# Conditioning sums with two buffers, then in pieces of 512 columns, and a mixing matrix turned in place: a two-layer hybrid encoder step on one core

## The chip, the core and the metric

The kernel runs on one core of a Trainium2 chip. The metric is the device time of one launch in microseconds (us); lower is better. TensorE (PE) does matmuls and transposes, VectorE (DVE) and ScalarE (ACT) do elementwise work, and SyncE (SP) and ScalarE each issue transfers on a queue of their own. PE accumulates in PSUM; everything else lives in on-chip buffers ("tiles") that are taken in turn from pools with a fixed number of buffers.

## What is computed

One step of a two-layer encoder for 1024 prompt rows and 32 sample rows with shared weights. All of it is float32.

```python
for i in range(2):
    mod = silu(c) @ w_ada[i] + b_ada[i]              # (1, 6*1024), one for prompt, one for sample
    sh1, sc1, gt1, sh2, sc2, gt2 = split(mod, 6)
    h = rmsnorm(x, g_norm[i, 0]) * (1 + sc1) + sh1
    if i == 0:                                       # spatial gating, chunks of T = 128 (sample: 32) rows
        u, v = split(gelu(h @ w_in), 2)              # 2048 columns each, 8 groups of 256
        v = rmsnorm(v, g_v)
        s = einsum('gij,bnjgd->bnigd', w_s * mask, v by chunk and group) + b_s
        mix = (u * s) @ w_out
    else:                                            # windowed means of 2, 4, 8, 16 rows, minus the row,
        mix = pool_mixer(h)                          # then a 256 x 256 map per group
    x = x + gt1 * rmsnorm(mix, g_norm[i, 1])
    h = rmsnorm(x, g_norm[i, 2]) * (1 + sc2) + sh2
    x = x + gt2 * rmsnorm(square(relu(h @ w_up[i])) @ w_down[i], g_norm[i, 3])
```

Each layer's `w_ada` is 1024 x 6144, 24 MB, and is read once for two conditioning vectors.

## The kernel before

**Tiles.** The 1056 rows lie transposed (features on partitions) in three tiles of 384, 384 and 288 columns. Large products are made from a high and a low part of each operand: `products` issues three matmuls per term, high x high, high x low and low x high. A weight piece of 128 x 1024 arrives in a `raw` buffer (3 of them), ACT copies its high part `wh` and VectorE subtracts to get `wl` (`do_w`); both take slots of `W` (16 slots, 8 pieces).

**Stages.** First the norms and the first products (`early`). Then the v stage: `v_order` lists 31 products of a 128-row block by a piece of 512 columns of v, 13 of the first two pieces, then 9 each of the third and the fourth. Then the gating stage: `mixes` lists six pairs of groups with the tiles that each runs over; one `sgu_item` per pair and tile (12 in all) makes u for two groups (`up`), gates it (`gate`) and multiplies by the output weights (`down`, held back until the next item's first product). Then both layers' FFN, with the pool mixer's work between.

**The stream.** All weights come in one list, `stream`, in the order in which `add_w`, `add_ada` and `add_x` append them; `some_ada(n)` puts n conditioning items between the weights. `issue` keeps three raw buffers loading, on SP's queue. `weave` runs after each product or so: it takes at most one item off the stream, unless `stream_waits` says that a planner's clock for VectorE (`time["dve"]`) is ahead of that for PE (`time["pe"]`). `need_w` forces everything ahead of a weight that a product needs.

**Conditioning.** The first 16 items go over PE (`do_ada_pe`). The other 80 go over VectorE (`do_ada`): an item is 512 rows by 256 columns of `w_ada`, two items make a slice. For both vectors, VectorE multiplies the rows by `csil` (silu of c) and adds into `aa`, a buffer of 2 x 256 columns of which there is one. The sum over the 128 partitions is PE's: `fold` multiplies by `pick` (a column of ones at a moving place) in four 32-row strips, collects four slices in a PSUM tile, and `fold2` transposes the lot and adds the bias (`ada_finish`). Folds are put off by `defer` and run in `run_deferred`; the first item of a slice forces the fold before it.

**Mixing matrix.** `sgu_group` loads a group's 128 x 128 matrix into `ws` (one buffer), transposes it on PE, copies it to `wt` (three buffers), clears a quarter (the mask), and loads the bias rows into `bs`, all loads on SP. `inputs`, ahead of a group's first products, loads v and scales the matrix by v's norm factors into `wr`.

The instructions of one engine stand in the order that the framework gives them, which isn't always that of the program. Elementwise helpers on VectorE have the line L79.

Of the kernel before, what the change touches and what calls it, by code (L numbers as in the profile page):

```python
# [9 lines left out]
F32 = mybir.dt.float32  # L10
# [24 lines left out]
def tile_stream_encoder_step(  # L35
# [78 lines left out]
    nc.vector.tensor_copy(onesr, one[:, :P])  # L114
    ones = onesr.bitcast(F32)

    pick = const.tile([P, 64], F32, name="pick")
    nc.vector.memset(pick, 0.0)
    nc.vector.memset(pick[:, 31:32], 1.0)
# [94 lines left out]
    def add_ada(l, j):  # L214

        sl, q = j // 2, j % 2
        stream.append(
            (
                "ada",
                (l, sl, q),  # L220
                w_ada[l][q * 512 : (q + 1) * 512, sl * 256 : (sl + 1) * 256].rearrange(
                    "(k p) f -> p k f", p=P
                ),
                (4, 256),
            )
        )

# [71 lines left out]

    def some_ada(n):  # L300
        for _ in range(min(n, len(rest))):
            add_ada(*rest.pop(0))

    for b in range(3):
        add_x(b)
# [34 lines left out]
    wdone = set()  # L340
    raws = {}
    loads = {}
    state = {"issued": 0, "next": 0, "raw": 0, "used": 0}
    deferred = []

    def in_raw(k):
# [84 lines left out]
        defer(fold)  # L431


    def do_ada(l, sl, q, r):
        if q == 0:
            ada_acc[0] = work.tile([P, NV, 256], F32, tag="aa", bufs=1, name=f"aa{l}_{sl}")
        aa = ada_acc[0]
        for c in range(4):
            for v in range(NV):
                w = r[:, c * 256 : (c + 1) * 256]  # L440
                k = csil[:, 4 * q + c, v : v + 1]
                if q == 0 and c == 0:
                    ts(aa[:, v, :], w, k, None, op0=ALU.mult)
                else:
                    stt(out=aa[:, v, :], in0=w, scalar=k, in1=aa[:, v, :], op0=ALU.mult, op1=ALU.add)
        if q == 0:
            return

        i = sl % 4

        def fold():

            if i == 0:
                ada_acc["ps"] = ps_ms(f"ada{l}_{sl}")
            pa = ada_acc["ps"]
            for c in range(4):
                v, h = c // 2, c % 2
                mm(
                    pa[32 * c : 32 * c + 32, :P],
                    pick[:, 31 - i : 63 - i],  # L460
                    aa[:, v, h * P : (h + 1) * P],
                    start=i == 0,
                    stop=i == 3,
                    tile_position=(0, 32 * c),
                    skip_group_check=True,
                )
            if i < 3:
                return
            s = t_m(f"adas{l}_{sl}")
            act(out=s[:, :P], in_=pa[:, :P], func=AF.Copy)  # L470

            def fold2():
                pb = ps_ms(f"adat{l}_{sl}")
                nc.tensor.transpose(pb[:, :P], s[:, :P], ident)
                ada_finish(
                    l,
                    sl - 3,
                    pb[:, :P].rearrange("p (v h m) -> p m h v", v=NV, h=2)[:, 0:4],
                )

            defer(fold2, 0.8)

        defer(fold, 0.3)

    def defer(step, us=None):

# [42 lines left out]
    def stream_step():  # L529

        k = state["next"]
        kind, key, ap, shape = stream[k]
        issue()
        run_deferred(force=kind == "ada" and key[2] == 0)
        r = raws.pop(k)
        if kind == "w":
            do_w(key, r)
        elif kind == "ada":
            (do_ada_pe if k < first_ada else do_ada)(*key, r)
        else:  # L540
            do_x(key, r)
        state["next"] += 1
        if in_raw(k):
            state["raw"] -= 1
        issue()

    def stream_waits():

        kind, key = stream[state["next"]][:2]
        if kind == "w":  # L550
            return bool(fillers) and wpos[key] > state["used"] + 5 and time["dve"] > time["pe"] + 1.0
        if kind == "ada" and deferred and key[2] == 0:
            return True
        return kind == "ada" and time["dve"] > time["pe"] + 0.5

    def need_w(key):
        state["used"] = max(state["used"], wpos[key])
# [3 lines left out]
        return witem[key]  # L561

    def need_ada(l, which):
        k = max(i for i, s in enumerate(stream) if s[0] == "ada" and s[1] == (l, which * 4 + 3, 1))
# [346 lines left out]
    v_order = [(1, 2)]  # L911
    v_order += [(p, b) for p in range(2) for b in range(3, 9)]
    v_order += [(p, b) for p in range(2, 4) for b in range(9)]
    for p, b in v_order:
        ps = ps_dn(f"pv{p}_{b}")
        v_mm(ps, p, b, range(KB))
        v_end(ps, p, b)
        if p == 2 and b < NT:
            with tc.issue_after(loads[("v", 2, 3)]):
                nc.sync.dma_start(xd[b], acc[b][:, :, HALO:])  # L920
        if p == 3 and b % 3 == 2:
            v_rms(b // 3)
        weave()
# [18 lines left out]
            yield False  # L942

    fillers.append(("state", sgu_state()))


    pending = []
# [28 lines left out]


    def sgu_group(g):
        raw = sgu.tile([P, P], F32, tag="ws", bufs=1, name=f"ws{g}")
        nc.sync.dma_start(raw, sgu_w_s[0, g])  # L980
        bb = sgu.tile([P, P], F32, tag="bs", bufs=3, name=f"bs{g}")
        nc.sync.dma_start(bb, sgu_b_s[0, g].partition_broadcast(P))
        pt = ps_ms(f"wsT{g}")
        nc.tensor.transpose(pt[:, :P], raw, ident)
        wt = sgu.tile([P, P], F32, tag="wt", bufs=3, name=f"wt{g}")
        nc.vector.tensor_copy(wt, pt[:, :P])
        nc.vector.memset(wt[64:P, 0:64], 0.0)
        return wt, bb

    def sgu_item(p, t, mix, after):  # L990
        gs, tiles = mixes[p]
# [5 lines left out]
        vls, wrs = {}, {}  # L997

        def inputs(g):
            wt, _ = mix[g]  # L1000
# [221 lines left out]
    def to_pool(st):  # L1222
# [4 lines left out]
        def run():  # L1227
# [269 lines left out]
```

## Time and profile before

| | |
|---|---|
| median of 3 runs | 2222.41 us (2219.92 to 2223.79) |
| the profiled execution's own time | 2220.61 us |
| its span, first to last instruction | 2218.8 us |
| PE busy | 2187.9 us (99%), 13488 matmuls |
| VectorE busy | 1404.1 us (63%) |
| ScalarE busy | 986.4 us (44%) |
| moved by transfers | 312.99 MB, mean 141 GB/s |

Rows of the profile give a start or a window in us from the span's start, a length, the engine, the line of the kernel, the operation, `out<-in` by the program's names, and in brackets the engine's idle time before it with what ended it. PEld is the load of a matmul's stationary side. A float32 matmul appears as two instructions.

### The profile page before, as it was taken

How to read it: one execution, taken by the hardware profiler on the slowest of the kernel's cores; microseconds unless marked ns; L12 is line 12 of the kernel's file. 1: busy time of each engine (PE TensorE's matmuls, PEld its weight loads, DVE VectorE, ACT ScalarE, POOL GpSimd, SP SyncE). 2: the span in 40 equal slices, each digit the busy share in tenths (PEclk: the TensorE clock that was granted, in tenths of full speed). 3: DMA queues.
4: the chain of work that ended last, by engine and by line, in shares of the span. 5: the costliest groups of instructions: out<-in, count | busy, mean ns of one | idle time of the engine just before them, and what ended most of it. 6: DMA issues, size and time to landing. Idle time of an engine off the chain costs nothing.

```text
span 2218.8 us, 33828 instructions
## 1 busy us (share of the span) xinstructions
PE 2187.9 (99%) x13488; PEld 2096.6 (94%) x13488; DVE 1404.1 (63%) x2646; ACT 986.4 (44%) x1675; POOL 0.7 (0%) x6
## 2 busy tenths in 40 slices
PE   7999999999999999999999999999999999999998
PEld 5777899999999999999999999999999999999998
DVE  4755656665869646676757869878765454433375
ACT  4633423133447553223445556666564542313354
POOL 0000000000000000000000000000000000000000
PEclk9999999999999999999999999999999999999999
DMA  8365533244436543334554556665454552312243
GB/s 299 123 199 196 176 112 126 78 148 126 135 98 194 162 143 124 114 109 125 154 170 140 165 162 187 184 190 155 147 162 140 153 154 64 96 29 77 92 124 110
DMA packets 369090, 312.99 MB, mean 141 GB/s; under 512 B 10818, under 2 KB 345098, under 8 KB 368932
## 3 DMA queue, kind: packets, MB, share of 16 engines
q1 hardware_dynamic: 368660, 310.74, 45.1%
q8 instruction: 105, 1.72, 0.3%
q14 instruction: 53, 0.43, 0.1%
q10 hardware_dynamic: 272, 0.10, 0.0%
HBM read 278.95 MB, written 31.84 MB: 140 GB/s over the span
## 4 chain that ended last, share of the span: by engine, by line
PE 92%; DVE 3%; DMA 3%; ACT 1%; issue 0%; SPq 0%; DVEq 0%; ACTq 0%
PE pf L803 11%; PE pf L804 11%; PE pf L805 11%; PE pg L803 11%; PE pg L804 11%; PE pg L805 11%; PE po L803 3%; PE po L804 3%; PE po L805 3%; PE pu L803 3%; PE pu L805 3%; PE pu L804 3%; PE pv L830 2%; PE pv L831 2%; PE pv L832 2%; DVE aa L79 2%
## 5 line engine op out<-in xcount | busy, mean ns | idle before, releaser
L803 PE MATMUL pg<-fh,wh_dn 128*128 128x384 f32 (+1 forms) x1536 | 499.2, 325 | 0.0
L803 PE MATMUL pf<-hh,wh_up 128*128 128x384 f32 (+1 forms) x1536 | 497.6, 324 | 0.6 <-ACT wh_up L372 0.6
L805 PE MATMUL pf<-hh,wl_up 128*128 128x384 f32 (+1 forms) x1536 | 495.8, 323 | 0.6 <-DVE wl_up L79 0.6
L804 PE MATMUL pf<-hl,wh_up 128*128 128x384 f32 (+1 forms) x1536 | 496.3, 323 | 0.0
L804 PE MATMUL pg<-fl,wh_dn 128*128 128x384 f32 (+1 forms) x1536 | 494.4, 322 | 0.0
L805 PE MATMUL pg<-fh,wl_dn 128*128 128x384 f32 (+1 forms) x1536 | 494.1, 322 | 0.0
L79 DVE TENSOR_TENSOR wl_up<-raw,wh_up 128x1024 fp32r<-128x1024 f32 x152 | 185.8, 1223 | 169.8 <-ACT wh_up L372 169.8
L803 PEld LDWEIGHTS pg<-fh,wh_dn 128*128 128x128 f32 x1536 | 288.5, 188 | 4.0 <-issue 2.4
L803 PEld LDWEIGHTS pf<-hh,wh_up 128*128 128x128 f32 x1536 | 288.2, 188 | 2.8 <-issue 1.4
L804 PEld LDWEIGHTS pg<-fl,wh_dn 128*128 128x128 f32 x1536 | 288.6, 188 | 0.7
L805 PEld LDWEIGHTS pf<-hh,wl_up 128*128 128x128 f32 x1536 | 288.2, 188 | 1.0 <-DVE wl_up L79 1.0
L805 PEld LDWEIGHTS pg<-fh,wl_dn 128*128 128x128 f32 x1536 | 288.6, 188 | 0.0
L804 PEld LDWEIGHTS pf<-hl,wh_up 128*128 128x128 f32 x1536 | 288.2, 188 | 0.4
L372 ACT ACTIVATE wh_up<-raw 128x1024 fp32r<-128x1024 f32 x152 | 161.0, 1059 | 281.5 <-PE pf L804 208.1
L79 DVE TENSOR_TENSOR acc<-acc,pg 128x384 f32<-128x384 f32 (+1 forms) x336 | 173.4, 518 | 141.1 <-PE pg L805 140.5
L372 ACT ACTIVATE wh_dn<-raw 128x1024 fp32r<-128x1024 f32 x152 | 161.0, 1060 | 210.6 <-PE pg L804 164.3
L79 DVE TENSOR_TENSOR wl_dn<-raw,wh_dn 128x1024 fp32r<-128x1024 f32 x152 | 185.9, 1223 | 89.3 <-ACT wh_dn L372 89.0
L79 DVE SCALAR_TENSOR_TENSOR aa<-raw,csil,aa 128x256 f32<-128x256 f32 x560 | 231.2, 478 | 1.8 <-DMA raw<-in_w_ada_dram 1.8
L1121 ACT ACTIVATE r<-pf 128x384 f32<-128x384 f32 (+1 forms) x192 | 86.6, 451 | 202.7 <-PE pf L805 199.3
L79 DVE TENSOR_TENSOR fl<-r,fh 128x384 fp32r<-128x384 f32 (+1 forms) x192 | 100.3, 522 | 105.1 <-ACT fh L957 103.5
L803 PE MATMUL pu<-hh,wh_u 128*128 128x384 f32 (+1 forms) x384 | 126.1, 328 | 0.0
L805 PE MATMUL pu<-hh,wl_u 128*128 128x384 f32 (+1 forms) x384 | 124.4, 324 | 0.8 <-DVE wl_u L79 0.8
(253 smaller groups left out, 2923.7 us busy)
## 6 DMA issues: line engine op xcount, KB each, us to landing
raw<-in_ffn_w_up_dram SPq DMA_DIRECT2D x152, 512.0 KB, 4.1
raw<-in_ffn_w_down_dram SPq DMA_DIRECT2D x152, 512.0 KB, 3.4
raw<-in_w_ada_dram SPq DMA_DIRECT2D x96, 512.0 KB, 4.2
raw<-in_sgu_w_in_dram SPq DMA_DIRECT2D x40, 512.0 KB, 4.1
xd<-acc SPq DMA_DIRECT2D x8, 1536.0 KB, 6.9
raw<-in_sgu_w_out_dram SPq DMA_DIRECT2D x24, 512.0 KB, 3.7
xo_r<-xd SPq DMA_DIRECT2D x32, 384.0 KB, 3.5
vd<-vt SPq DMA_DIRECT2D x32, 256.0 KB, 2.4
```

What stands on the lines that cost most here:

```text
L79: return op(out, *args, **kw)
L372: act(out=wh, in_=r, func=AF.Copy)
L803: mm(ps[:, :n], wh, rh, start=i == 0, stop=False)
L804: mm(ps[:, :n], wh, rl, start=False, stop=False)
L805: mm(ps[:, :n], wl, rh, start=False, stop=i == last)
L830: mm(ps[:m, :], a_h, wh[:, o : o + 512], start=k == 0, stop=False)
L831: mm(ps[:m, :], a_h, wl[:, o : o + 512], start=False, stop=False)
L832: mm(ps[:m, :], a_l, wh[:, o : o + 512], start=False, stop=k == KB - 1)
L1121: act(out=r[:, :n], in_=ps[:, :n], func=AF.Relu)
```

## The change

The sums `aa` get two buffers of 512 columns. The first 24 of the 80 VectorE items (l = 0, up to column 5120) stay narrow: a slice takes one buffer. The other 56 become wide: 256 rows by 512 columns, four items to a slice, and a slice takes both buffers, one per vector. `state["folds"]` counts buffers that wait for their fold, and the first item of a slice forces the folds only if its buffers aren't free (`folds_hold`). A wide fold has 256 columns in each strip, and two slices fill a PSUM tile; two transposes follow.

In the v stage folds are deferred by 3.0 us of the planner's clock instead of 0.3, the planner's clock for VectorE is set to 4.0 us ahead of PE's as the stage begins, and the items between the weights are shared out as 8, 8, 8, 8, 8 instead of 10, 8, 8, 6, 8.

The mixing matrix is loaded into `wt` itself (two buffers, `ws` is gone), transposed from there and copied back. This turn and the scaling into `wr` follow the group's first products. The bias load goes to ACT's queue, into one of two buffers. In the pool mixer two of the four group weights, which used an `aa` buffer, use one of the three `x3` buffers.

```diff
-            csil32 = work.tile([P, NV, 256], F32, tag="aa", bufs=1, name="csil32").rearrange(
+            csil32 = work.tile([P, NV, 256], F32, tag="aa", bufs=2, name="csil32").rearrange(
...
+    def add_wide(l, j):
+
+        sl, q = j // 4, j % 4
+        ada_last[(l, 2 * sl)] = ada_last[(l, 2 * sl + 1)] = len(stream)
+        stream.append(
+            (
+                "wide",
+                (l, sl, q),
+                w_ada[l][q * 256 : (q + 1) * 256, sl * 512 : (sl + 1) * 512].rearrange(
+                    "(k p) f -> p k f", p=P
+                ),
+                (2, 512),
+            )
+        )
...
-    rest += [(0, j) for j in range(16, 48)]
-    some_ada(10)
+    rest += [(add_ada, 0, j) for j in range(16, 40)] + [(add_wide, 0, j) for j in range(40, 48)]
+    some_ada(8)
...
-    rest += [(1, j) for j in (*range(8, 16), *range(8), *range(16, 48))]
+    rest += [(add_wide, 1, j) for j in (*range(8, 16), *range(8), *range(16, 48))]
...
-            some_ada((6, 8)[n])
+            some_ada(8)
...
-    def do_ada(l, sl, q, r):
+
+    def do_ada(l, sl, q, r, w):
+        nq = w // 128
         if q == 0:
-            ada_acc[0] = work.tile([P, NV, 256], F32, tag="aa", bufs=1, name=f"aa{l}_{sl}")
+            aas = [
+                work.tile([P, 512], F32, tag="aa", bufs=2, name=f"aa{l}_{sl}_{w}_{i}")
+                for i in range(nq // 2)
+            ]
+            ada_acc[0] = [aas[v * nq // 4][:, v * w % 512 :][:, :w] for v in range(NV)]
         aa = ada_acc[0]
-        for c in range(4):
+        for c in range(8 // nq):
             for v in range(NV):
...
-        if q == 0:
+        if q < nq - 1:
             return
...
+        ni = 8 // nq
+        h = w // 2
+        i = sl % ni
+        state["folds"] += nq // 2
...
             for c in range(4):
-                v, h = c // 2, c % 2
                 mm(
-                    pa[32 * c : 32 * c + 32, :P],
-                    pick[:, 31 - i : 63 - i],
-                    aa[:, v, h * P : (h + 1) * P],
+                    pa[32 * c : 32 * c + 32, :h],
+                    pick[:, 3 - i : 35 - i],
+                    aa[c // 2][:, c % 2 * h : (c % 2 + 1) * h],
                     start=i == 0,
-                    stop=i == 3,
+                    stop=i == ni - 1,
...
-                nc.tensor.transpose(pb[:, :P], s[:, :P], ident)
...
+                for j in range(h // P):
+                    x = slice(j * P, (j + 1) * P)
+                    nc.tensor.transpose(pb[:, x], s[:, x], ident)
...
-        defer(fold, 0.3)
+        defer(fold, fold_lag[0])
+
+    fold_lag = [3.0]
...
-        run_deferred(force=kind == "ada" and key[2] == 0)
+        run_deferred(force=folds_hold(kind, key))
...
+    def folds_hold(kind, key):
+
+        need = {"ada": 1, "wide": 2}.get(kind)
+        return need is not None and key[2] == 0 and state["folds"] + need > 2
...
-        if kind == "ada" and deferred and key[2] == 0:
+        if folds_hold(kind, key):
             return True
-        return kind == "ada" and time["dve"] > time["pe"] + 0.5
+        return kind in ("ada", "wide") and time["dve"] > time["pe"] + 0.5
...
     v_order += [(p, b) for p in range(2, 4) for b in range(9)]
+    time["dve"] = time["pe"] + 4.0
     for p, b in v_order:
...
     fillers.append(("state", sgu_state()))
 
+    fold_lag[0] = 0.3
...
     def sgu_group(g):
-        raw = sgu.tile([P, P], F32, tag="ws", bufs=1, name=f"ws{g}")
-        nc.sync.dma_start(raw, sgu_w_s[0, g])
-        bb = sgu.tile([P, P], F32, tag="bs", bufs=3, name=f"bs{g}")
-        nc.sync.dma_start(bb, sgu_b_s[0, g].partition_broadcast(P))
-        pt = ps_ms(f"wsT{g}")
-        nc.tensor.transpose(pt[:, :P], raw, ident)
-        wt = sgu.tile([P, P], F32, tag="wt", bufs=3, name=f"wt{g}")
-        nc.vector.tensor_copy(wt, pt[:, :P])
-        nc.vector.memset(wt[64:P, 0:64], 0.0)
-        return wt, bb
+        wt = sgu.tile([P, P], F32, tag="wt", bufs=2, name=f"wt{g}")
+        nc.sync.dma_start(wt, sgu_w_s[0, g])
+        bb = sgu.tile([P, P], F32, tag="bs", bufs=2, name=f"bs{g}")
+        nc.scalar.dma_start(bb, sgu_b_s[0, g].partition_broadcast(P))
+
+        def turn():
+            pt = ps_ms(f"wsT{g}")
+            nc.tensor.transpose(pt[:, :P], wt, ident)
+            nc.vector.tensor_copy(wt, pt[:, :P])
+            nc.vector.memset(wt[64:P, 0:64], 0.0)
+
+        return wt, bb, [turn]
...
+        def factors(g):
+            wt, _, turn = mix[g]
+            while turn:
+                turn.pop()()
             wr = wrs[g] = t_m(f"wr{g}_{t}")
...
             products(ps, n, up_terms(("u", p, g, k), t))
+            if k == 0:
+                factors(g)
...
-                    wg = work.tile([P, 2, 256], F32, tag="aa", bufs=1, name=f"wg{t}_{g}")
+                    wg = t_x(f"wg{t}_{g}", [P, 2, 256])
```

More of the change, by code (lines that the diff above doesn't have):

```diff
@@ L115, in tile_stream_encoder_step @@
     ones = onesr.bitcast(F32)
-    pick = const.tile([P, 64], F32, name="pick")
+    pick = const.tile([P, 36], F32, name="pick")
     nc.vector.memset(pick, 0.0)
-    nc.vector.memset(pick[:, 31:32], 1.0)
+    nc.vector.memset(pick[:, 3:4], 1.0)
     inv = const.tile([P, 16], F32, name="inv")
@@ L216, in add_ada @@
         sl, q = j // 2, j % 2
+        ada_last[(l, sl)] = len(stream)
         stream.append(
@@ L224, in add_ada @@
                 (4, 256),
+            )
+        )
+    ada_last = {}
+    def add_wide(l, j):
[9 more added lines that the diff above has]
+                (2, 512),
             )
@@ L301, in some_ada @@
         for _ in range(min(n, len(rest))):
-            add_ada(*rest.pop(0))
+            add, l, j = rest.pop(0)
+            add(l, j)
     for b in range(3):
@@ L342, in tile_stream_encoder_step @@
     loads = {}
-    state = {"issued": 0, "next": 0, "raw": 0, "used": 0}
+    state = {"issued": 0, "next": 0, "raw": 0, "used": 0, "folds": 0}
     deferred = []
@@ L431, in do_ada_pe @@
         defer(fold)
-    def do_ada(l, sl, q, r):
+    def do_ada(l, sl, q, r, w):
+        nq = w // 128
         if q == 0:
-            ada_acc[0] = work.tile([P, NV, 256], F32, tag="aa", bufs=1, name=f"aa{l}_{sl}")
+            aas = [
[3 more added lines that the diff above has]
+            ada_acc[0] = [aas[v * nq // 4][:, v * w % 512 :][:, :w] for v in range(NV)]
         aa = ada_acc[0]
-        for c in range(4):
+        for c in range(8 // nq):
             for v in range(NV):
-                w = r[:, c * 256 : (c + 1) * 256]
-                k = csil[:, 4 * q + c, v : v + 1]
+                x = r[:, c * w : (c + 1) * w]
+                k = csil[:, 8 // nq * q + c, v : v + 1]
                 if q == 0 and c == 0:
-                    ts(aa[:, v, :], w, k, None, op0=ALU.mult)
+                    ts(aa[v], x, k, None, op0=ALU.mult)
                 else:
-                    stt(out=aa[:, v, :], in0=w, scalar=k, in1=aa[:, v, :], op0=ALU.mult, op1=ALU.add)
-        if q == 0:
+                    stt(out=aa[v], in0=x, scalar=k, in1=aa[v], op0=ALU.mult, op1=ALU.add)
+        if q < nq - 1:
             return
-        i = sl % 4
+        ni = 8 // nq
+        h = w // 2
+        i = sl % ni
+        state["folds"] += nq // 2
         def fold():
+            state["folds"] -= nq // 2
             if i == 0:
@@ L466, in fold @@
                 )
-            if i < 3:
+            if i < ni - 1:
                 return
             s = t_m(f"adas{l}_{sl}")
-            act(out=s[:, :P], in_=pa[:, :P], func=AF.Copy)
+            act(out=s[:, :h], in_=pa[:, :h], func=AF.Copy)
             def fold2():
                 pb = ps_ms(f"adat{l}_{sl}")
-                nc.tensor.transpose(pb[:, :P], s[:, :P], ident)
[L475 to L479, printed above, removed]
+                for j in range(h // P):
+                    x = slice(j * P, (j + 1) * P)
+                    nc.tensor.transpose(pb[:, x], s[:, x], ident)
+                if w == 256:
+                    y = pb[:, :P].rearrange("p (v h m) -> p m h v", v=NV, h=2)
+                    ada_finish(l, sl - 3, y[:, 0:4])
+                else:
+                    y = pb[:, :256].rearrange("p (h v a m) -> p m a h v", h=2, v=NV, a=2)
+                    for n in range(2):
+                        ada_finish(l, 2 * (sl - 1 + n), y[:, n])
             defer(fold2, 0.8)
-        defer(fold, 0.3)
+        defer(fold, fold_lag[0])
+    fold_lag = [3.0]
     def defer(step, us=None):
@@ L537, in stream_step @@
             do_w(key, r)
+        elif kind == "wide":
+            do_ada(*key, r, 512)
         elif kind == "ada":
-            (do_ada_pe if k < first_ada else do_ada)(*key, r)
+            if k < first_ada:
+                do_ada_pe(*key, r)
+            else:
+                do_ada(*key, r, 256)
         else:
@@ L563, in need_ada @@
     def need_ada(l, which):
-        k = max(i for i, s in enumerate(stream) if s[0] == "ada" and s[1] == (l, which * 4 + 3, 1))
+        k = max(ada_last[(l, which * 4 + i)] for i in range(4))
         while state["next"] <= k:
@@ L999, in inputs @@
         def inputs(g):
-            wt, _ = mix[g]
             vl = vls[g] = t_x(f"vl{g}_{t}", [P, 3, 256])
```

## The prediction

> **What bounds the kernel now.** I read the page first, then PE's waits, then the count of matmuls in stretches of 10 us, then single rows of the timeline. The page names the bound:
>
> ```profile
> span 2218.8 us, 33828 instructions
> PE 2187.9 (99%) x13488; PEld 2096.6 (94%) x13488; DVE 1404.1 (63%) x2646; ACT 986.4 (44%) x1675; POOL 0.7 (0%) x6
> ```
>
> TensorE is busy for 99% of the span, so no engine can be relieved to much effect; the change can win only what TensorE loses by waiting, and what it spends on instructions that the change makes fewer. The waits of PE that touch the changed code (who waits, for whom: us in total, times, longest):
>
> ```profile
> PE ada L458 <- DVE aa L79: 5.0, 3, 2.3
> PE pv L831 <- DVE wl_v L79: 1.3, 3, 0.5
> PE wsT L984 <- DMA ws<-in_sgu_w_s_dram: 1.1, 2, 0.5
> ```
>
> The first is the fold of a conditioning sum (`ada`), which reads the sum `aa` that VectorE is still making. This list undercounts, since a matmul counts as busy until its drain ends. A better measure is how many `pv` matmuls fit into 10 us (columns: window, length, busy us and count of PE, PEld, DVE, ACT, granted clock, DMA share, GB/s; `pv` instructions alone):
>
> ```profile
> 90.00:100.00 10.00, 10.00 (x45) 8.12 (x45) 0.00 (x0) 2.64 (x6) 1.00 0.08 28
> 120.00:130.00 10.00, 9.71 (x43) 7.64 (x42) 0.00 (x0) 2.52 (x6) 1.00 0.35 111
> 140.00:150.00 10.00, 6.82 (x24) 4.47 (x23) 0.67 (x1) 1.31 (x3) 0.83 0.54 164
> 150.00:160.00 10.00, 9.26 (x40) 6.99 (x39) 0.00 (x0) 2.52 (x6) 1.00 0.96 343
> 190.00:200.00 10.00, 7.22 (x30) 4.27 (x28) 0.67 (x1) 2.61 (x6) 1.00 0.38 123
> 200.00:210.00 10.00, 8.66 (x33) 5.99 (x34) 0.00 (x0) 0.00 (x0) 1.00 0.68 218
> ```
>
> 45 fit into an undisturbed window and 43 where one fold lies in it, so one takes about 0.23 us. Against 43, 45, 42 and 44 (one, none, one and a half and half a fold) the four disturbed windows lack 19, 5, 12 and 11: 47 matmuls, 47 x 0.23 = 10.8 us. Both places are where the v stage changes to its next piece of 512 columns. The other losses, all instructions counted:
>
> ```profile
> 250.00:260.00 10.00, 8.72 (x56) 7.24 (x54) 8.90 (x30) 6.24 (x10) 0.00 (x0) 1.00 0.76 223
> 260.00:270.00 10.00, 9.43 (x54) 9.43 (x55) 8.15 (x17) 5.73 (x8) 0.00 (x0) 1.00 0.82 258
> 900.00:930.00 30.00, 29.87 (x196) 28.17 (x195) 19.25 (x46) 5.51 (x11) 0.00 (x0) 1.00 0.36 106
> 1060.00:1110.00 50.00, 48.76 (x294) 46.86 (x292) 37.94 (x74) 20.98 (x32) 0.00 (x0) 1.00 0.53 158
> ```
>
> That is 1.28 + 0.57 = 1.85 us at the start of the gating stage and 0.13 + 1.24 = 1.37 us in the first layer's FFN. With the 10.8 us, 14.0 us of waiting lie within the change's reach.
>
> **Two buffers in the v stage.** Why PE loses time there is seen in VectorE's rows and PE's beside them:
>
> ```profile
> 125.76 0.62 DVE L79 TENSOR_SCALAR aa<-raw,csil 128x256 f32<-128x256 f32 x2 [5.40 <-PE ada L458]
> 126.29 5.63 DVE L79 SCALAR_TENSOR_TENSOR aa<-raw,csil,aa 128x256 f32<-128x256 f32 x14
> 141.07 0.71 PE L830 MATMUL pv<-wh_v,hh 128*128 128x512 f32 x2
> 144.05 0.48 PE L458 MATMUL ada<-aa,pick 128*32 128x128 f32 x4 [2.27 <-DVE aa L79]
> ```
>
> A sum takes VectorE from 125.76 to 131.92, 6.2 us, and before it VectorE stood idle for 5.40 us, because the one buffer is free only when PE has folded the sum before. VectorE could keep up, but the sums fall behind, and when the v stage needs the weights of its next piece, which lie behind those sums in the stream, everything is forced out at once: PE reaches the fold 2.27 us early, and the weights are loaded and split later still. The change gives the next sum a second buffer, defers each fold by 3.0 us of the planner's clock, starts the planner's VectorE clock only 4.0 us ahead of PE's, and puts 8 sum items instead of 10 ahead of the third piece. There are 13 products between the start of this loop and the third piece and one stream item after each, so 8 sums and the first weights fit, where 10 did not. For the fourth piece there are 9 products for 8 sums and 4 weights: the sums fit, the weights just about; W_SLOTS and the three raw buffers are unchanged. I take 2.0 of the 10.8 us to stay, at the fourth piece; the bounds are 0 and 10.8. Saved: 8.8 us. What is late next there is the weights' own chain of load, ACT copy and DVE subtraction.
>
> The 1.85 us at the start of the gating stage come from the same backlog (PE waits there for `aa`, for a split weight and for the mixing matrix); I take 1.4 us as saved, bounds 0 and 1.85.
>
> In 140:150 the granted clock is 0.83, which is half speed for 3.4 us. I count it as a consequence of the wait and so as saved, within the 19 matmuls. [...]
>
> **Fewer folds.** Each fold is eight PE instructions. What one costs PE, for 128 columns and, by its nearest relative (the first stage's conditioning matmuls, same stationary shape, 256 columns), for 256:
>
> ```profile
> L458 PE MATMUL ada<-aa,pick x320: 269/296/423, 104.0 to 1947.8; 128*32 128x128 f32 x160
> 913.65 0.34 PE L805 MATMUL pg<-fh,wl_dn 128*128 128x384 f32 x1
> 913.91 0.43 PE L458 MATMUL ada<-aa,pick 128*32 128x128 f32 x8
> 914.27 0.45 PE L803 MATMUL pg<-fh,wh_dn 128*128 128x384 f32 x1
> 914.56 0.33 PE L804 MATMUL pg<-fl,wh_dn 128*128 128x384 f32 x1
> 37.47 0.39 PE L832 MATMUL pv<-wh_v,hl 128*128 128x512 f32 x1
> 37.79 0.64 PE L404 MATMUL ada<-raw,csil 128*32 128x256 f32 x8
> 38.36 0.50 PE L831 MATMUL pv<-wl_v,hh 128*128 128x512 f32 x1
> 38.70 0.40 PE L832 MATMUL pv<-wh_v,hl 128*128 128x512 f32 x1
> ```
>
> From 913.65 to 914.56 are two steps of 0.17 (the pitch of 384 columns, as between 522.45 and 522.62 below), so the fold takes 0.91 - 0.35 = 0.56 us. From 37.47 to 38.70 are two steps of 0.23, so the wide one takes 1.23 - 0.46 = 0.77 us. The 320 instructions are 40 folds. Afterwards 24 items in the v stage make 12 narrow folds and 56 items make 14 wide ones: 12 x 0.56 + 14 x 0.77 = 17.5 us in place of 40 x 0.56 = 22.4: 4.9 us saved, and PE has nothing else to do meanwhile, so all of it counts. Were the wide fold as cheap as the narrow one, it would be 2.9 us more; were it twice as dear (1.12 us), 4.9 us less. Against it stand more transposes of the folded sums: 10 before, afterwards 3 + 7 x 2 = 17. Their price is that of the mixing matrix's, which have the same shape:
>
> ```profile
> 522.45 0.34 PE L805 MATMUL pu<-hh,wl_u 128*128 128x384 f32 x1
> 522.62 0.28 PE L984 MATMUL wsT<-ident,ws 128*128 128x128 f32 x1
> 522.65 0.42 PE L803 MATMUL pu<-hh,wh_u 128*128 128x384 f32 x1
> 522.92 0.34 PE L804 MATMUL pu<-hl,wh_u 128*128 128x384 f32 x1
> 486.55 0.33 PE L984 MATMUL wsT<-ident,ws 128*128 128x128 f32 x1 [0.51 <-DMA ws<-in_sgu_w_s_dram]
> ```
>
> 522.45 to 522.92 less two steps of 0.17 is 0.13 us; seven more cost 0.9 us.
>
> **Sums of 512 columns.** The wide sums need half as many VectorE instructions per column. The row nearest to a 512-column one, and those of the mixing matrix:
>
> ```profile
> 280.24 0.74 DVE L79 SCALAR_TENSOR_TENSOR vst<-vst,rv,gvb 32x512 f32<-32x512 f32 x1
> L986 DVE COPY wt<-wsT x12: 272/284/292, 253.7 to 593.0; 128x128 f32<-128x128 f32 x12
> L79 DVE TENSOR_SCALAR wr<-wt,rv x72: 222/281/289, 255.0 to 650.3; 128x128 f32<-128x128 f32 x64, 32x32 f32<-32x32 f32 x8
> DMA to landing us min/median/max: 1.7/2.6/8.3
> L79 DVE TENSOR_TENSOR wl_up<-raw,wh_up 128x1024 fp32r<-128x1024 f32 x152 | 185.8, 1223 | 169.8 <-ACT wh_up L372 169.8
> ```
>
> An item is 4 x 0.74 = 3.0 us, where a narrow one is half of 6.2, 3.1 us, at most (back to back, 14 narrow instructions took 0.40 each, so the wide ones may come to less than 0.74). This is off PE's path except in 1060:1110, where VectorE is busy for 37.94 of 50 us and a wait for split weights shows. A wide sum holds both buffers, so its successor waits for the fold as now, but every fourth item, not every second. I take 0.9 of the 1.37 us, bounds 0 and 1.37.
>
> **The mixing matrix.** Its load goes straight into `wt`, the turn is issued behind the group's first 24 products, 24 x 0.17 = 4.1 us after the load can be awaited, against 2.6 us to landing: its waits on PE (486.55) go. Half of their 1.1 us I have counted already in 250:260, so 0.5 us more, bounds 0 and 1.1. SyncE loses the bias loads to ACT's queue. On SyncE the load of `wt` now waits for VectorE's last scaling by the matrix of two groups ago, and the weight loads queue behind it; on ACT the bias load waits for the gate two groups ago, with weight copies and Gelu behind. Both waits end with the previous group's last item, ahead of a whole item of products, so I cost them at nothing, up to one 2.6 us landing for each of six pairs of groups if that cover is gone. Pool weights in an `x3` buffer wait for a window sum and not for a fold; the pool stage shows no PE wait, cost nothing, at most 3 x 2.6 us.
>
> **The sum**, against the profiled execution's 2220.61 us (span 2218.8): -8.8 - 1.4 - 0.5 - 0.9 - 4.9 + 0.9, and +1.0 for small new waits (taken near nothing, since PE waits nowhere else) = -14.6 us. The median of the runs is 2222.41, 1.8 us above the profiled one; taken from it, 2207.8, rounded to 2208.
>
> **Rivals.** *The weights are late by themselves.* For it: 150:160 and 200:210 lack 16 matmuls behind the fold, while split weights arrive. Then only 3.8 of the 10.8 us come back, 5 less: 2213.
> *The second buffer isn't what decides*, and the forced folds remain, because the order of the stream or the slots hold the sums up. Against it: the 5.40 us idle rows name the fold. Then the 8.8 us stay: 2217.
> *The gates wait, and it becomes slower.* The scaling by the mixing matrix (`wr`) moves behind the first products. For the second group of each of the 12 items (3 + 3 + 1 + 1 + 2 + 2) only the other 24 products, 4.1 us, cover it. If VectorE has two weight subtractions (1.22 each) and a wide item (3.0) ahead, then copy and three scalings (0.28 + 0.84) end after 6.6 us: 2.5 us late, 12 x 2.5 = 30 us, and without the 1.0 for small waits 2222.4 - 15.6 + 30 = 2237. From 1.3 us each (15.6 / 12) it is no longer faster, from 1.7 slower by more than 0.2%. For it: VectorE is 8 to 9 tenths busy in 250:270. [...]
>
> **How the numbers follow.** A measurement of this kernel tells about 0.2% from no change, 4.4 us: faster is below 2218, slower above 2226.8. Forecast 0.58 (own range 2203 to 2212), late weights 0.14 (2213), buffer not decisive 0.10 (2217, half of it within 0.2%), gates waiting 0.18 (0.04 within 0.2%, 0.14 slower). So faster 0.77, same 0.09, slower 0.14. The range reaches down to 2200 (all 14.0 us back and wide folds at 0.56) and up to 2222, where half of the gates' price eats the gain; beyond lie about 2 in 10.
>
> **What would show it.** Right: 40 folds become 26; `pv` counts of 42 or more in every window of the v stage; no VectorE idle of 5 us behind `ada L458`; no half clock near 145 us; no wait on `wsT`; the FFN rows unchanged. Wrong: `psp` waiting on `wr`; waits on `wl_v` as long as now; an ACT or SyncE queue blocked at a bias or `wt` load while PE waits for a weight.

## The result, and the profile after

| | before | after |
|---|---|---|
| median of the runs | 2222.80 us (2219.92 to 2223.79, 4 runs) | 2204.39 us (2203.96 to 2205.38, 4 runs) |
| ratio | | 0.9918, interval 0.9903 to 0.9933 |
| the profiled execution | 2220.61 us | 2204.23 us |
| its span | 2218.8 us | 2202.4 us |

The change makes the kernel 18.4 us faster by the medians and 16.4 us by the two profiled executions, where 14.6 were forecast. First the page of after, the lines that answer to the first ones of before:

```profile
span 2202.4 us, 33445 instructions
PE 2179.8 (99%) x13383; PEld 2095.2 (95%) x13383; DVE 1378.1 (63%) x2439; ACT 986.7 (45%) x1675; POOL 0.7 (0%) x6
```

PE's busy time fell by only 8.1 us although the span fell by 16.4: the other half was idle time. PE's waits of after, as the list gives them (who waits, for whom: us in total, times, longest):

```profile
PE rowT L180 <- DMA row<-in_g_norm_dram: 4.9, 1, 4.9
PE ada L424 <- DMA raw<-in_w_ada_dram: 2.8, 2, 2.0
PE rowT L182 <- ACT row L178: 2.1, 1, 2.1
PE pb_h L686 <- ACT r_h L684: 1.9, 1, 1.9
PE rowT L180 <- DMA row<-in_b_ada_dram: 1.0, 1, 1.0
PE adat L441 <- ACT adas L436: 1.0, 2, 0.5
PE pn_r_2x L749 <- ACT xt L1258: 0.3, 1, 0.3
PE rowT L180 <- DMA row<-in_sgu_g_v_dram: 0.3, 1, 0.3
PE pv L876 <- ACT pv L889: 0.2, 1, 0.2
PE yT L1500 <- ACT yo L1501: 0.2, 1, 0.2
```

The 5.0 us for `aa`, the 1.3 for `wl_v` and the 1.1 for `ws` are gone, and what is left lies nearly all ahead of the v stage. The `pv` matmuls in the windows that were shown of before (same columns):

```profile
90.00:100.00 10.00, 9.71 (x43) 7.76 (x42) 0.00 (x0) 2.63 (x6) 1.00 0.35 116
120.00:130.00 10.00, 9.71 (x43) 7.47 (x42) 0.00 (x0) 1.93 (x5) 1.00 1.01 319
140.00:150.00 10.00, 10.00 (x45) 7.32 (x44) 0.68 (x1) 2.85 (x7) 1.00 0.31 92
150.00:160.00 10.00, 10.00 (x45) 8.19 (x45) 0.00 (x0) 2.43 (x6) 1.00 0.13 52
190.00:200.00 10.00, 9.71 (x42) 6.62 (x40) 0.67 (x1) 2.66 (x7) 1.00 0.66 198
200.00:210.00 10.00, 10.00 (x45) 8.23 (x44) 0.00 (x0) 2.62 (x6) 1.00 0.46 154
```

Where 24, 40, 30 and 33 fitted, 45, 45, 42 and 45 do, and the granted clock in 140:150 is 1.00 instead of 0.83. The windows of the later losses, all instructions:

```profile
250.00:260.00 10.00, 10.00 (x64) 9.96 (x63) 9.40 (x29) 5.05 (x8) 0.00 (x0) 1.00 0.69 235
260.00:270.00 10.00, 10.00 (x63) 9.88 (x62) 9.90 (x23) 1.98 (x4) 0.00 (x0) 1.00 0.44 128
900.00:930.00 30.00, 30.00 (x197) 29.34 (x197) 11.89 (x18) 8.25 (x16) 0.00 (x0) 1.00 0.35 103
1060.00:1110.00 50.00, 50.00 (x294) 49.30 (x293) 33.66 (x52) 18.37 (x25) 0.00 (x0) 1.00 0.57 168
```

PE is busy throughout. VectorE is at 9.90 of 10 in 260:270. The group of the folds; then, from the view of the tile `wr` (the matrix scaled for the gates), what PE's weight loads ahead of its readers waited for; then from the timeline a wide fold among its neighbours:

```profile
L488 PE MATMUL ada<-aa,pick x208: 272/379/404, 90.2 to 1931.5; 128*32 128x256 f32 x56, 128*32 128x128 f32 x48
```
```profile
  DVE wr L79: 0.3, 1
```
```profile
871.39 0.34 PE L851 MATMUL pg<-fh,wl_dn 128*128 128x384 f32 x1
871.66 0.64 PE L488 MATMUL ada<-aa,pick 128*32 128x256 f32 x8
872.23 0.45 PE L849 MATMUL pg<-fh,wh_dn 128*128 128x384 f32 x1
872.51 0.33 PE L850 MATMUL pg<-fl,wh_dn 128*128 128x384 f32 x1
```

208 instructions are 26 folds. A weight load for the gates waited for `wr` once, 0.3 us; in the list above no matmul waits for it. From 871.39 to 872.51 less two steps of 0.17 is 0.78 us for a wide one (0.77 forecast).

Four points cut the span into stages: the first product of the v stage behind the norms, the first `pu`, the last `po`, the end. The table holds the differences, read from single rows of the timeline of each kernel's profile, and will be used for every experiment. Each row is one execution: those of p_turn, v_noclock and m_once were the shortest of their kernels, those of v_plain, f_held and f_sp the longest.

| kernel | front | v stage | gating stage | rest |
|---|---|---|---|---|
| before | 69.7 | 181.8 | 420.9 | 1546.3 |
| after | 72.5 | 171.7 | 416.7 | 1541.5 |
| p_two | 69.7 | 171.9 | 417.7 | 1544.6 |
| p_wide | 69.1 | 171.9 | 423.5 | 1541.7 |
| p_turn | 70.5 | 180.3 | 419.2 | 1546.1 |
| v_one | 73.1 | 172.8 | 418.0 | 1541.3 |
| v_plain | 70.8 | 171.8 | 424.0 | 1541.5 |
| v_share10 | 71.8 | 171.9 | 422.9 | 1541.3 |
| v_noclock | 71.4 | 171.6 | 416.7 | 1541.5 |
| f_held | 72.0 | 172.0 | 416.5 | 1541.4 |
| f_sp | 72.2 | 171.7 | 416.4 | 1541.5 |
| after_again | 72.0 | 171.7 | 416.5 | 1541.3 |
| m_once | 69.4 | 171.9 | 417.0 | 1541.3 |
| m_once_again | 71.1 | 171.9 | 417.0 | 1541.5 |

Before to after: +2.8 - 10.1 - 4.2 - 4.8 = -16.3. Three stages gained, the front lost.

### The profile page after: what moved, and what is told of

It reads as the page before. It is cut to its first block, busy times and chain, and to the rows that moved or that the text cites. A ratio compares the mean times of both kernels' runs of the same rounds, so it can differ in the third digit from the quotient of the medians.

```text
span 2202.4 us, 33445 instructions
## 1 busy us (share of the span) xinstructions
PE 2179.8 (99%) x13383; PEld 2095.2 (95%) x13383; DVE 1378.1 (63%) x2439; ACT 986.7 (45%) x1675; POOL 0.7 (0%) x6
## 4 chain that ended last, share of the span: by engine, by line
PE 97%; DMA 1%; ACT 1%; DVE 1%; issue 0%; SPq 0%; DVEq 0%; ACTq 0%
PE pf L849 11%; PE pf L850 11%; PE pf L851 11%; PE pg L849 11%; PE pg L850 11%; PE pg L851 11%; PE pu L849 3%; PE pu L851 3%; PE pu L850 3%; PE po L849 3%; PE po L850 3%; PE po L851 3%; PE pv L876 3%; PE pv L877 2%; PE pv L878 2%; PE psp L1096 1%
## 5 line engine op out<-in xcount | busy, mean ns | idle before, releaser
L79 DVE SCALAR_TENSOR_TENSOR aa<-raw,csil,aa 128x512 f32<-128x512 f32 (+1 forms) x364 | 204.3, 620 | 6.0 <-DMA raw<-in_w_ada_dram 5.8
L849 PE MATMUL po<-ush,wh_o 128*128 128x384 f32 (+1 forms) x384 | 124.1, 323 | 0.0
```

The costliest lines, as they stand in the source:

```text
L79: return op(out, *args, **kw)
L849: mm(ps[:, :n], wh, rh, start=i == 0, stop=False)
```

## The experiments

**Which part wins what.** Three kernels, each meant to hold one part. p_two has two buffers and the planner's part (clock, deferral, shares of 8), with all sums narrow and the matrix in its place but turned at once (the pool weights' other buffer goes along, here and in p_wide):

```diff
-            ada_acc[0] = work.tile([P, NV, 256], F32, tag="aa", bufs=1, name=f"aa{l}_{sl}")
+            ada_acc[0] = work.tile([P, NV, 256], F32, tag="aa", bufs=2, name=f"aa{l}_{sl}")
...
-        defer(fold, 0.3)
+        defer(fold, fold_lag[0])
...
-    some_ada(10)
+    some_ada(8)
...
+    time["dve"] = time["pe"] + 4.0
```

> Two buffers alone: the changed v stage (two buffers, deferral by 3.0, the planner's clock, the shares of 8), with all sums in 256 columns; the mixing matrix is loaded into its place but turned at once, and the bias stays on SyncE's queue. If the second buffer and the order in the v stage are what gives the time back, the 10.8 us lost there and most of the 1.85 us behind it return, 40 folds remain: 12 us faster than before, 2211 us. If the wide sums and the fewer folds carry the gain, it is less than 6 us: above 2217.

Measured: 2206.9 us (2204.96 to 2208.66), ratio 0.9936 (0.9921 to 0.9951), 4 us less than expected. Its v stage is as short as in after, its rest 3.1 us longer: that is what the wide folds, with their transposes, are worth there.

p_wide has the wide sums alone, on top of before's shares, deferral and forced folds (the matrix again in its place and turned at once):

```diff
+    rest += [(add_ada, 0, j) for j in range(16, 40)] + [(add_wide, 0, j) for j in range(40, 48)]
...
+        return need is not None and key[2] == 0 and state["folds"] > 0
...
+    fold_lag = [0.3]
```

> Wide sums alone: pieces of 512 columns as in the change, but one slice at a time, shares of 10, 8, 8, 6, 8, the planner's clock and the deferral of before; the matrix turned at once, the bias on SyncE's queue. If a fold costs PE 0.56 us and a wide one 0.77 whatever else happens, 40 folds to 26 give 4.9 us, seven transposes more take 0.9, and the FFN's 1.4 us of waits go: 5.4 us faster than before, 2217 us, with the waits of the v stage as before. If folds are hidden somewhere, 1.4 us: 2221.

Measured: 2207.23 us (2206.31 to 2208.03), ratio 0.9937 (0.992 to 0.9953). The expectation was wrong in the main point: the v stage fell to 171.9 all the same, since its narrow slices, each of one 512-column buffer, take two physical buffers in turn. It loses 6.8 us more in the gating stage than after, where PE waits for the gates' v rows and the granted clock falls to 0.66 in 270:280:

```profile
PE psp L1086 <- DMA vl<-vd: 4.3, 2, 3.6
```

p_turn has the mixing matrix's part alone:

```diff
+        wt = sgu.tile([P, P], F32, tag="wt", bufs=2, name=f"wt{g}")
+        nc.sync.dma_start(wt, sgu_w_s[0, g])
...
+        nc.scalar.dma_start(bb, sgu_b_s[0, g].partition_broadcast(P))
...
+            if k == 0:
+                factors(g)
```

> Mixing matrix alone: the change to the group's matrix and bias on the kernel before, sums as before. The waits at the transposes go, 1.1 to 2.3 us. In the changed kernel the stage before the v stage ends 3.0 us later than before; if that comes from the bias loads on ACT's queue at 4.8 us, it shows here too and the sum is 1 us slower, 2223.5; if it comes from something else, 2 us faster, 2220.5.

Measured: 2221.77 us (2218.11 to 2224.58), ratio 1.0001 (0.9991 to 1.001). The gating stage is 1.7 us shorter in the profile, as the waits on `wsT` are gone; no gain shows in the time. Its v stage is 1.5 us shorter as well, without the 1.7 us that before's PE waits there for split weights; one execution doesn't tell whether that is the matrix's doing. The parts don't add: 14.0 + 13.7 us and nothing by the medians, where the whole change brings about 18. The two parts that gain win the same 10 us of the v stage.

**The buffer or the planner, in the v stage.** v_one is after with one buffer for narrow slices:

```diff
-                work.tile([P, 512], F32, tag="aa", bufs=2, name=f"aa{l}_{sl}_{w}_{i}")
+                work.tile([P, 512], F32, tag=f"aa{i}", bufs=1, name=f"aa{l}_{sl}_{w}_{i}")
...
-        return need is not None and key[2] == 0 and state["folds"] + need > 2
+        return need is not None and key[2] == 0 and state["folds"] + need > (2 if need > 1 else 1)
```

> The changed kernel with the narrow sums in one buffer, as before, and everything else of the change (planner's clock, deferral by 3.0, shares of 8, wide sums, matrix). If the second buffer itself gives the v stage its time back, PE waits for folds at the third and fourth piece again: 6 to 11 us slower than the changed kernel, 2210 to 2215 us. If the planner's part of the change does it, 2204 as the changed kernel. A forecast between: the sums start 20 us earlier by the planner's clock and have 8 items for 13 products, so one buffer might just do.

Measured: 2205.88 us (2204.15 to 2207.76), ratio 0.9927 (0.991 to 0.9943). The v stage takes 172.8 us, 1.1 more than in after. VectorE's waits behind the fold in the v stage (70:252 of before, 75:245 of the others), of before, of v_one and of after in turn:

```profile
DVE aa L79 <- PE ada L458: 55.3, 9, 15.0
```
```profile
DVE aa L79 <- PE ada L488: 47.5, 8, 15.6
```
```profile
DVE aa L79 <- PE ada L488: 30.6, 3, 15.6
```

With one buffer VectorE stands idle behind the folds nearly as long as before, 47.5 us, and PE loses almost nothing. The idle time that the prediction read as the fault is harmless by itself. That the loss comes when the backlog is then forced out ahead of a weight is argued from the rows of before; no run tries the forcing alone.

v_plain is the other half, two buffers without the planner's part:

```diff
-    some_ada(8)
+    some_ada(10)
...
-            some_ada(8)
+            some_ada((6, 8)[n])
...
-    fold_lag = [3.0]
+    fold_lag = [0.3]
...
-        return need is not None and key[2] == 0 and state["folds"] + need > 2
+        return need is not None and key[2] == 0 and state["folds"] > 0
...
-    time["dve"] = time["pe"] + 4.0
```

> The changed kernel without the planner's part: shares of 10, 8, 8, 6, 8, deferral by 0.3, the planner's VectorE clock left alone, the fold before each new slice put ahead of it; two buffers for the narrow sums, wide sums and the matrix as changed. The run with wide sums alone had no wait left in the v stage though it had none of the planner's part. If the second buffer decides, this is no slower than the changed kernel: 2200 to 2205 us, with 42 or more v matmuls in every 10 us. If the planner's part matters where buffers are two, a wait of 2 us or more stands again at 140 and 200 us: 2210.

Measured: 2208.13 us (2206.67 to 2209.96), ratio 0.9939 (0.9924 to 0.9953). The v stage is free of waits (171.8), so either cure alone suffices there. (v_plain's stream is held only by a fold that waits, where that of before is held by the transpose behind it as well; this was not tried by itself.) What is lost lies at the start of the gating stage, 7.3 us against after in this profile; by the medians v_plain is 3.7 us slower than after.

**What keeps the start of the gating stage free.** v_share10 is after with the shares of before alone, v_noclock is after without clock and deferral:

```diff
-    some_ada(8)
+    some_ada(10)
...
-            some_ada(8)
+            some_ada((6, 8)[n])
```

> The changed kernel with one part of the planner's changes put back: 10, 8, 8, 6 and 8 conditioning slices between the weights instead of 8 each; the clock set at the start of the v stage and the longer deferral of the folds stay. If the share-out is what keeps the start of the gating stage free of waits, the gating stage is 424 us again instead of 416.5, with TensorE waits on u, vl or weights there, and the time is 2204 + 5 = about 2209 us. If the clock and the deferral do it, the stage stays at 416.5 to 418 and the time is 2203 to 2205 us. The v stage stays at 172 us by both.

```diff
-    fold_lag = [3.0]
+    fold_lag = [0.3]
...
-    time["dve"] = time["pe"] + 4.0
```

> The changed kernel with the other part of the planner's changes put back: no setting of VectorE's clock at the start of the v stage and folds deferred by 0.3 instead of 3.0; the shares of 8 stay. If the share-out decides the start of the gating stage, that stage is 416.5 to 418 us and the time 2203 to 2205 us. If the clock and the deferral decide it, the stage is 424 us with waits on u or the gates' inputs, and the time about 2208 us. With two narrow buffers the v stage stays at 172 us in both cases.

Measured: v_share10 2208.29 us (2205.29 to 2211.24), ratio 0.9942 (0.9929 to 0.9956); v_noclock 2204.38 us (2203.0 to 2205.24), ratio 0.9924 (0.9911 to 0.9938). It is the share-out; with two buffers the clock and the deferral do nothing that a run shows. The four times of v_share10 lie far apart; by the medians the share-out is worth 3.9 us, in the profiles 6.2. v_share10's waits of PE in 235:300 and two of its windows, all instructions:

```profile
PE psp L1096 <- DMA vl<-vd: 2.3, 1, 2.3
PE pu L849 <- ACT u L1084: 0.9, 1, 0.9
```
```profile
250.00:260.00 10.00, 6.81 (x33) 6.22 (x32) 7.42 (x19) 7.01 (x10) 0.00 (x0) 0.77 0.78 259
260.00:270.00 10.00, 10.00 (x54) 9.97 (x53) 8.09 (x17) 1.98 (x4) 0.00 (x0) 0.89 0.29 86
```

3.2 us of waiting, and behind it half clock (matmuls of 512 columns then start 0.43 us apart instead of 0.23, as from 146.34 to 146.77 in before) for 2 x (0.23 + 0.11) x 10 = 6.8 us, which costs another 3.4: together about the 6.2 us by which its stage is longer. Why, is seen on ACT: the last copy of a weight for `u`, the last of the first output weights, and the first activation of `u`, first in after, then in v_share10.

```profile
237.19 1.06 ACT L392 ACTIVATE wh_u<-raw 128x1024 fp32r<-128x1024 f32 x1 [2.29 <-DMA raw<-in_sgu_w_in_dram]
248.29 1.06 ACT L392 ACTIVATE wh_o<-raw 128x1024 fp32r<-128x1024 f32 x1 [0.40 <-DMA raw<-in_sgu_w_out_dram]
252.79 0.87 ACT L1084 ACTIVATE u<-pu 128x384 f32<-128x384 f32 x2
```
```profile
243.18 1.06 ACT L392 ACTIVATE wh_u<-raw 128x1024 fp32r<-128x1024 f32 x1 [3.39 <-DMA raw<-in_sgu_w_in_dram]
253.46 1.06 ACT L392 ACTIVATE wh_o<-raw 128x1024 fp32r<-128x1024 f32 x1 [1.10 <-DMA raw<-in_sgu_w_out_dram]
257.35 0.87 ACT L1084 ACTIVATE u<-pu 128x384 f32<-128x384 f32 x2
```

26 sum items lie ahead of the gating stage's weights instead of 24. The weights come 5 to 6 us later, ACT takes their copies ahead of `u`, and the v rows are asked for behind them on SyncE (at 248.36 instead of 244.88). The two items are also the first two of a wide sum, which holds both buffers; before, with 26 narrow ones, PE lost only 1.85 us there. Number and width are not separated by a run.

**The front.** After starts its v stage 2.8 us later than before. f_held holds the first matrix and bias loads behind the load of a later weight and puts the bias on SyncE's queue, f_sp does only the latter, after_again changes nothing:

```diff
+        with tc.issue_after(loads[("v", 2, 0)]):
+            nc.sync.dma_start(wt, sgu_w_s[0, g])
+            nc.sync.dma_start(bb, sgu_b_s[0, g].partition_broadcast(P))
```

> The changed kernel with the first matrix and bias loads held back on SyncE's queue until the third v piece's first load is issued. If the bias loads on ACT's queue and the matrix loads among the first weights cost the front its 3.0 us, they return: 2201.4 us against 2204.4, and no PE wait of 2 us at the conditioning matmul near 33 us, no half clock behind it. If the front's loss is chance of one execution, 2204.4.

```diff
-        nc.scalar.dma_start(bb, sgu_b_s[0, g].partition_broadcast(P))
+        nc.sync.dma_start(bb, sgu_b_s[0, g].partition_broadcast(P))
```

> The changed kernel with the bias loads back on SyncE's queue and nothing held back. If the bias load on ACT's queue at 4.8 us puts the front back, its end (first v product after the norms at 72.5 us, 69.7 before) comes 1 to 3 us earlier and the time is 2202 to 2203; if it is chance, 2204.

> The changed kernel once more, for a second profile of its front. If the 3 us that the front lost are the kernel's, the half clock near 35 us and the wait at the conditioning matmul near 33 us come again; if they are chance of one execution, the first v product after the norms stands elsewhere than 72.5 us by over 1 us. The time 2204.4 either way.

Measured: f_held 2203.02 us (2202.36 to 2203.71), ratio 0.9919 (0.9904 to 0.9934); f_sp 2201.12 (2200.64 to 2203.77), 0.9909 (0.9894 to 0.9924); after_again 2203.75 (2202.81 to 2205.07), 0.9919 (0.9904 to 0.9934). The front is 72.0 to 72.2 in the three profiles, so neither moving the early loads nor moving the bias shortens it there. In the times, three of f_sp's four are 2200.6 to 2201.4, where all of after, after_again and f_held lie above 2202.3. So far the fronts were 69.1 to 69.7 where the matrix is turned at once and 70.5 to 73.1 where it is turned behind the first products, so m_once takes the turn's place back, with the bias on SyncE's queue as in f_sp, and m_once_again is the same kernel a second time:

```diff
-        nc.scalar.dma_start(bb, sgu_b_s[0, g].partition_broadcast(P))
-
-        def turn():
-            pt = ps_ms(f"wsT{g}")
-            nc.tensor.transpose(pt[:, :P], wt, ident)
...
+        nc.sync.dma_start(bb, sgu_b_s[0, g].partition_broadcast(P))
+        pt = ps_ms(f"wsT{g}")
+        nc.tensor.transpose(pt[:, :P], wt, ident)
...
-            if k == 0:
-                factors(g)
```

> The changed kernel with the mixing matrix turned as soon as it is loaded (still in its own place, bias on SyncE's queue), so without the part that puts the turn behind the first products. If the turn's place is what makes the front 2 to 3 us longer in every kernel that has it, the v stage's product of 120 matmuls begins at 69.5 instead of 72.2, the v stage and the gating stage stay at 171.7 and 416.5 us, and the time is 2201.4 - 2.6 = about 2199 us; the waits of the mixing matrix (12 x 0.12 against 3.63 in the kernel before) don't come back, since the load is asked for far ahead. If the front varies for another reason, the front is 72 and the time 2201 to 2204. If the turn at once waits for its load, there are waits on wsT of up to 2 us and the time is 2203 to 2206.

> The kernel with the matrix turned at once a second time, unchanged, for the front alone. If the place of the turn decides the length of the front, the v stage's product of 120 matmuls begins at 69.1 to 69.7 us again, as in the four profiles so far that turn at once. If the front's length is drawn anew in each execution (five times of the first study were 2201.5, 2201.6 and three of 2203.5 to 2203.8), it can as well be 70.5 to 73, as in the eight profiles that turn behind the first products; the median lies between 2201.5 and 2203.8 by both.

Measured: 2203.5 us (2201.51 to 2203.8), ratio 0.9919 (0.9906 to 0.9933), and 2203.35 (2201.42 to 2204.01), 0.9919 (0.9905 to 0.9932); 2199 was expected if the turn's place decides. The first profile had a front of 69.4, the second one of 71.1. The window 34:38 of the first and of the second:

```profile
34.00:38.00 4.00, 4.00 (x27) 2.53 (x29) 3.06 (x7) 1.99 (x3) 0.00 (x0) 1.00 0.57 192
```
```profile
34.00:38.00 4.00, 4.00 (x19) 2.34 (x18) 2.98 (x7) 1.99 (x3) 0.00 (x0) 0.60 0.55 173
```

One kernel, much the same waits ahead (1.04 and 0.77 us, 1.12 and 0.77), and the clock falls in one execution and not in the other: 2 x 0.40 x 4 = 3.2 us at half speed cost 1.6 of the 1.7 us. The ten times of this kernel lie in two groups, three at 2201.4 to 2201.6 and seven at 2203.3 to 2204.0. So a good part of the front's length is drawn anew in each execution. In the profile of after the clock fell there too (0.57 in 34:38), and the wait for `raw` ahead of it was 2.0 us instead of 1.0.

Added up in this way over windows of 4 us from 14 to 46, the half speed accounts for most of the column of fronts. It is 3.4 us in before, p_two, p_wide, p_turn, v_plain, v_noclock and m_once, whose fronts are 69.1 to 71.4; 6.8 or 6.9 us in after, after_again, f_held, f_sp, v_share10 and m_once_again, 71.1 to 72.5; and 10.2 us in v_one, 73.1. It needn't lie at 34:38. These are f_sp's windows:

```profile
18.00:22.00 4.00, 3.51 (x24) 1.61 (x27) 0.07 (x1) 0.87 (x2) 0.00 (x0) 0.50 1.10 350
34.00:38.00 4.00, 3.80 (x27) 2.17 (x28) 1.85 (x3) 2.28 (x3) 0.00 (x0) 1.00 0.73 236
```

With equal half speed, the kernels that turn the matrix behind the first products still have the longer fronts, by 1.4 and 1.0 us in the mean: 70.5 to 71.4 against 69.1 to 69.7, and 71.8 to 72.5 against the 71.1 of m_once_again. So the turn's place goes with about 1 us of the front and does not decide the rest. By which wait, and whether the turn's place or the bias's queue makes half speed likelier, stays open. Turned at once, the matrix has no wait for its load either. No variant is shown faster than after: the interval of f_sp overlaps with that of after.

## Why the prediction held, and where it was off

**The v stage: mis-sized by 1.3 us.** 8.8 were forecast, 10.1 came. The term that failed is the 2.0 us left at the fourth piece; the weights were in time there too. *The weights are late by themselves* is refuted with it: nothing was done to their chain, and no `wl_v` wait is left. The price of this rival was also misread: the 16 matmuls that it names are 3.7 us that would stay, so 7.1 us would come back and not 3.8.

**Its cause: half right.** A second buffer removes the loss (v_plain, p_wide). But the rival *the second buffer isn't what decides* has its share: with one buffer and the planner's part, the loss is gone but for 1.1 us (v_one). Wrong in that rival was its price, that the 8.8 us would stay. Which of shares, clock and deferral does it in v_one wasn't tried. The sign "no VectorE idle of 5 us behind the fold" failed while the forecast held: 30.6 us of such idle time are left, in three places (15.6, 5.4 and 9.6 us), and PE has no wait from 75 to 245.

**Start of the gating stage and mixing matrix: mis-sized by 1.2 us.** 1.4 + 0.5, with 8 x 0.56 - 4 x 0.77 = 1.4 for its folds and -0.3 for transposes, make 3.0 us; measured 4.2. 1.7 of it is the matrix by p_turn's profile, where I had counted 0.5 and half of 1.1. That the shares alone keep this start free I hadn't seen: I used them in the v stage, where they aren't needed.

**FFN: mis-sized by 1.0 us.** 0.9 of waits, 20 x 0.56 - 10 x 0.77 = 3.5 for the folds less 0.6 for transposes make 3.8; measured 4.8. The waits went wholly (1.37, not 0.9), and by p_two and after the wide folds are worth 3.1 there, with their transposes, instead of 2.9; the other 0.3 us are not accounted for.

**Folds and transposes: right.** Read between their neighbours like the one above, 12 narrow folds take 0.55 to 0.56 us and 14 wide ones 0.77 to 0.78: 17.5, as forecast. The transposes of folded sums cost about 0.8 us more, 0.9 forecast.

**New waits: forecast 1.0, measured 0.3.** *The gates wait* comes to 0.3 us, once (the row for `wr` above), not 12 x 2.5. VectorE was as full as that rival needs, 9.90 of 10 us in 260:270; yet the gates came in time.

**The front: a term that was missing.** +2.8 us in the profiles. The three stages, with that 0.3 in them, brought 1.3 + 1.2 + 1.0 = 3.5 us more than forecast, and the 1.0 for new waits wasn't needed besides; the front took 2.8: -14.6 - 3.5 - 1.0 + 2.8 = -16.3, the difference of the stages. About 1.7 of the 2.8 us is half speed, 6.9 us of it instead of 3.4; the rest is what the kernels with the later turn have in common. The half speed differs from one execution to the next (3.4 us in the front of m_once, 6.8 in that of m_once_again), so the medians may differ by more or less than this. That the sum came within 2 us of the measured gain is in part luck: the stages and the new waits came out 4.5 us better than forecast, the front 2.8 us worse.

**The clock near 145 us: right for the sum.** With the fold's wait gone the half speed is gone: the granted clock is 1.00 in 140:150 of after, where it was 0.83 in before.

## What to carry to other kernels

Idle time of an engine behind a buffer isn't yet a loss (in v_one VectorE stood idle for 47.5 us behind the folds, and PE waited 0.4 us in 75:245): look for the point at which the backlog is forced out, and move that or empty the backlog ahead of it; here two cures overlapped, and their gains didn't add. Two items more or fewer ahead of a stage's first weights were worth 6 us in the profiles and 4 us by the medians, so count what lies in the queue ahead of a stage change. What a small group of instructions costs a busy engine is read from the starts of its neighbours, before and behind: that price held to a few hundredths of a us.

## What the runs showed of the hardware

A wait of about 2.2 us was followed by a lower granted clock in one run and not in another. In before a wait of 2.19 us was followed by a granted clock of 1.00 in 200:210 (the window stands in the prediction):

```profile
199.70 0.41 PE L458 MATMUL ada<-aa,pick 128*32 128x128 f32 x4 [2.19 <-DVE aa L79]
```

In p_turn a wait of 2.20 us, at the same fold, was followed by 0.84:

```profile
199.31 0.41 PE L458 MATMUL ada<-aa,pick 128*32 128x128 f32 x4 [2.20 <-DVE aa L79]
```
```profile
200.00:210.00 10.00, 10.00 (x40) 7.63 (x40) 6.43 (x11) 3.06 (x4) 0.00 (x0) 0.84 0.74 236
```

2 x 0.16 x 10 is 3.2 us of half speed in this window. Added up in the same way, half speed was 3.4 us in 140:150 of before, 6.8 in 250:270 of v_share10, and 3.4, 6.8 to 6.9 or 10.2 in the fronts. What decides whether the clock falls behind a wait isn't shown: m_once and m_once_again are one kernel with much the same waits, and had 3.4 and 6.8 us of half speed in their fronts; their ten times lie in two groups about 2 us apart. As an estimate from these rows, a wait of 2 us on PE costs 2.0 to 3.7 us: itself, and half of 3.4 us where the clock falls.
